# Reordering the head of a two-layer hybrid trunk on one Trainium2 core

## The chip, the core and the metric

The kernel runs on one core of one Trainium2 chip. Its engines run side by side and wait for each other by semaphores: TensorE (PE in the profile; its weight loads are PEld), VectorE (DVE), ScalarE (ACT), GpSimd (POOL) and SyncE (SP), which here issues nearly all DMA loads. The metric is the device time of one execution in microseconds. Lower is better.

## The reference, cut to what matters

The reference is a trunk of two layers on 256 tokens of 1024 channels, all in float32. A vector `c` gives six modulation vectors for each layer; a layer is a token mixer and a convolutional FFN, each on a modulated, normalised input.

```python
for l in range(2):
    mod = c @ mod_w[l] + mod_b[l]            # 6 vectors of 1024
    sh1, sc1, g1, sh2, sc2, g2 = split(mod, 6)
    h = rmsnorm(x, norm1_g[l]) * (1 + sc1) + sh1
    x = x + g1 * mixer(h, positions, ...)    # proj = h @ w_in; rotary embedding; two attentions; gates
    h = rmsnorm(x, norm2_g[l]) * (1 + sc2) + sh2
    x = x + g2 * conv_ffn(h, ...)
return rmsnorm(x, final_g)
```

Only the start of the first layer matters here: the first modulation columns (shift and scale, 128 channels at a time), the sum of squares over the channels of `x`, the modulated input `h`, and its product with the first part of `w_in`. The rotary embedding needs tables of sines and cosines of the positions, and the attentions need masks; both are first used much later, near 50 us.

## The kernel before, in words

Channels lie on the 128 partitions, so `x` is a tile of 8 blocks of 128 channels by 256 tokens. Every float32 product is made of three matmuls at a reduced float format: a high and a low part of each operand, high times high, high times low, low times high (`mm3`). So each weight block that is loaded (`raw`) is split: ScalarE makes the high part (`whi`, an `Identity` activation with rounding, `split_hi`), VectorE the low part (`wlo`, a subtraction, `split`). Likewise the input: `ht` (VectorE) is `x` times gain times the row factor, `hh` (ScalarE) its high part with the shift added, `hl` (VectorE) its low part.

The work is a list of steps (`add(...)`, executed by `run_steps`), each with the weight tiles that it consumes. All weights go through SyncE's queue, in the order of use, into rings of tiles. A load into a tile that was in use waits on that queue until the tile is free. `pin("V", "A", "PE")` keeps the instructions of VectorE, ScalarE and TensorE in the order of the program from there on; without it a scheduler may move them.

The head (the part of the run that the change touches) does this:

- five loads on SyncE: positions, frequencies, a part of the small vectors `vc`, and `x` in two halves; then the weight stream;
- constants by memset and iota; `begin` squares `x` on ScalarE, half by half, and adds the squares on VectorE; `tables` makes the rotary angles with some twenty-five steps of 16 elements on VectorE and two sines on ScalarE; `masks` makes the masks;
- `go0`: modulation column 0. `mod_mm(k, half, raw)` multiplies one half of its rows (eight matmul records on the TensorE timeline), and copies the result out to `mods` after the second half. The sums of the squares over channels are matmuls with a column of ones (`sum_rows`: two matmuls, four records). `rstd` makes the row factor on VectorE and GpSimd (a power). `mod_fin` transposes the column, spreads the row factor over partitions (`rstd_rows`), reduces the column (`modr`), adds the bias (`mod`), makes the gain, and then `ht`, `hh`, `hl` of that block of channels;
- `go(k)`, for k = 0 to 7: the rows of weight block k. Its matmuls come in two halves of tokens (`rows_block` with js = (0,) and (1,): three pairs each, high-high, low-high, and last high-low, which needs `wlo`), then twelve for the other heads (`rows`). Between them stand `mod_fin(k + 1)`, which makes the next block of `h`, the splitting of the next weights, and at the end `mod_both(k + 2)`, a later modulation column.

`go(0)` makes modulation column 1 ahead of its first half:

```python
if k == 0:
    mod_both(1, *mc[:2])
    mc = mc[2:]
...
state["split_hi"](2)
rows_block(S["idx"], k, w, 0, ..., (0,))
mod_fin(k + 1)
rows_block(S["idx"], k, w, 0, ..., (1,))
rows(k, w, 1)
state["split"](2)
if mc:
    mod_both(k + 2, *mc)
```

Of the kernel before, what the change touches and what calls it, by code (L numbers as in the profile page):

```python
# [16 lines left out]
P = 128  # L17
# [10 lines left out]
# buffers: of raw weights, of split weights (pairs), of small work tiles; tiles lent to early loads  # L28
# [4 lines left out]
# how many weight tiles are split ahead of a step  # L33
# [5 lines left out]
# modulation vectors: those summed on the vector engine, those spread over the mixer, over the FFN  # L39
# [4 lines left out]
# parts of a vector that fill the gaps around the norms, and the places of their loads  # L44
# [3 lines left out]
# engines that keep the order of the program between the layers  # L48
# [21 lines left out]
def hybrid_trunk(ctx: ExitStack, tc: tile.TileContext, xT, vec, fbias, pos, invf,  # L70
# [8 lines left out]
    class Engine:  # L79
        """an engine whose instructions stay in the order of the program while pinned"""  # L80
# [42 lines left out]
    # ------------------------------------------------- the stream of weights  # L123
    # steps run in order; the tiles they name are loaded, and split, ahead of them
# [10 lines left out]
    def run_steps():  # L135
        """chunks (source, columns, kind): "w" and "m" pass through the ring "raw", "s" through
        the tiles FIRST and "g", four at a time, through the tile of the gates, both from the
        epoch on that the fourth entry names, and not before the other chunks that stand less than
        the fifth entry behind it"""
# [95 lines left out]
    # ---------------------------------------------------------------- inputs  # L235
# [3 lines left out]
    nc.sync.dma_start(posi, pos)  # L239
    ivf = const.tile([P, 8], F32, name="ivf")  # L240
    nc.sync.dma_start(ivf, invf)
    nc.sync.dma_start(vc[:, :V_L + V_CW], vec[:, :V_L + V_CW])
# [4 lines left out]
    # ------------------------------------------------------------- constants  # L247
# [3 lines left out]
    V.tensor_scalar(ident, jp, 0.0, None, op0=OP.is_equal)  # L251
    tri = const.tile([P, 3 * P], F32, name="tri")
    V.memset(tri[:, 0:P], 0.0)
    V.memset(tri[:, 2 * P:], 1.0)
    causal = const.tile([P, T], F32, name="causal")
    V.memset(causal[:, 0:P], 0.0)
    chunked = const.tile([P, T], F32, name="chunked")
    V.memset(chunked, 0.0)
    V.memset(chunked[0:64, P + 64:], NEG)
# [12 lines left out]
    V.tensor_copy(cpad[:, :, 0], vc[:, V_C:V_C + KT])  # L272
# [4 lines left out]
    V.memset(LF, 0.0)  # L277
    cum = const.tile([P, T], F32R, name="cum")
    V.memset(f(cum), 0.0)
# [19 lines left out]
    def tables():  # L299
        """rotary tables, cos | cos and -sin | sin, one row per token"""  # L300
# [16 lines left out]
        for c in (PI_1, PI_2, PI_3):  # L317
            for n in (nh, nt):
                V.scalar_tensor_tensor(ang, n, -c, ang, op0=OP.mult, op1=OP.add)
        PI = TWO_PI / 2  # L320
# [5 lines left out]
        A.activation(ss[:, :, 8:16], ang, AF.Sin)  # L326
        V.scalar_tensor_tensor(nt, ang, -1.0, ang, op0=OP.mult, op1=OP.min)
        V.tensor_scalar(nt, nt, PI / 2, None, op0=OP.add)
        A.activation(cc[:, :, 0:8], nt, AF.Sin)
# [5 lines left out]
    # ------------------------------------------------------------ modulation  # L335
# [8 lines left out]
    def mod_vector(l, v, kind=(("m",),), vector=False):  # L344
        """one of the six vectors, eight row blocks: summed over the blocks in PSUM, or on the vector
        engine with the last sum over rows in PSUM; a column tile for each 256 columns"""
# [42 lines left out]
    # ---------------------------------------------------------- normalisation  # L389
# [59 lines left out]
    def h_stream(l, rb, shift, hh, hl):  # L449
        """the blocks one after the other, the high part of each ahead of the low part of the one before"""  # L450
        t = h_high(l, 0, rb, shift, hh)
        for k in range(KT):
            n = h_high(l, k + 1, rb, shift, hh) if k + 1 < KT else None
            h_low(l, k, t, shift, hh, hl)
            t = n
            yield
# [7 lines left out]
    def rows_block(tiles, k, w, base, split, hh, hl, js=(0, 1), low_last=False):  # L464
        """one 128-row block of a token-major projection"""
# [770 lines left out]
```

## Time and profile before

| what | us |
|---|---|
| median of 3 runs | 819.35 |
| lowest and highest run | 817.91, 819.90 |
| span of the profiled execution (first to last instruction) | 817.1 |
| TensorE busy in it | 795.0 |
| VectorE, ScalarE, GpSimd busy in it | 643.1, 498.7, 8.9 |

The profiled execution is known by its span alone: no time of its own beyond that is listed. The lowest run is 0.8 us above that span, the median 2.25. Times in the rows are microseconds from the start of the span. A row of the timeline has the start, the duration, the engine, the line of the code (a helper, for nearly all), the operation, the tile that it writes and those that it reads, their shape, and how many instructions were merged into it; in brackets stands how long the engine was idle before and what released it.

### The profile page before, as it was taken

The page shows a single profiled execution, that of the slowest core. Times are in us where ns is not written, and L with a number is a line of the kernel's source. Part 1 is how long each engine was busy: PE and PEld are TensorE (multiplying, and loading weights), DVE is VectorE, ACT ScalarE, POOL GpSimd, SP SyncE. Part 2 cuts the span into 40 slices and gives each one's busy share as a digit, 9 for nine tenths or more (in the row PEclk, how much of TensorE's full clock was granted, in tenths as well). Part 3 has the DMA queues.
Part 4 walks back from the last instruction along what each step waited for, and adds up shares of the span by engine and source line. Part 5 has one row for each costly group of instructions (what it writes and reads, how often), then busy time and mean ns, then how long its engine had stood idle before and what let it go on. Part 6 is the DMA issues. An engine that isn't in the chain of part 4 may idle for free.

```text
span 817.1 us, 16972 instructions
## 1 busy us (share of the span) xinstructions
PE 795.0 (97%) x6644; PEld 758.1 (93%) x6644; DVE 643.1 (79%) x1338; ACT 498.7 (61%) x905; POOL 8.9 (1%) x19
## 2 busy tenths in 40 slices
PE   4999999999999999999999999999999999999997
PEld 2899988989899999999989999999998999999996
DVE  6689998879689998898666799766876877676763
ACT  4476567645476665667654666766555765666664
POOL 2000000000000000000000000000000000000000
PEclk9999999999999999999999999999999999999998
DMA  8955867867969899997525456433693665566611
GB/s 325 409 152 175 282 209 234 261 230 264 413 248 322 314 319 333 322 331 248 168 71 151 140 189 209 128 125 108 196 373 100 210 190 191 185 183 183 193 38 52
DMA packets 51776, 179.24 MB, mean 219 GB/s; under 512 B 6256, under 2 KB 6384, under 8 KB 51696
## 3 DMA queue, kind: packets, MB, share of 16 engines
q1 hardware_dynamic: 51696, 178.15, 64.7%
q8 instruction: 52, 0.85, 0.4%
q14 instruction: 28, 0.23, 0.1%
HBM read 177.08 MB, written 1.05 MB: 218 GB/s over the span
## 4 chain that ended last, share of the span: by engine, by line
PE 51%; issue 24%; DVE 2%; DMA 1%; POOL 0%; ACT 0%; POOLq 0%; DVEq 0%; ACTq 0%
PE psA L89 30%; PE psB L89 19%; PE psM L89 2%; PE psC L89 1%; DVE y L89 1%; DVE wlo L89 1%; DMA raw<-wout 1%; DVE raw L89 0%; POOL rstd L417 0%; ACT whi L89 0%; DVE hl L89 0%; DVE kzl L89 0%; DVE yout L89 0%; POOLq L1231 0%; DVE ql L89 0%
## 5 line engine op out<-in xcount | busy, mean ns | idle before, releaser
L89 DVE TENSOR_TENSOR wlo<-raw,whi 128x1024 fp32r<-128x1024 f32 (+3 forms) x252 | 293.4, 1168 | 79.9 <-ACT whi L89 78.4
L89 ACT ACTIVATE whi<-raw 128x1024 fp32r<-128x1024 f32 (+3 forms) x252 | 254.4, 1014 | 157.4 <-PE psB L89 58.2
L89 PE MATMUL psB<-hh,whi 128*128 128x256 f32 x768 | 215.7, 282 | 0.0
L89 PE MATMUL psB<-hl,whi 128*128 128x256 f32 x768 | 215.4, 281 | 0.0
L89 PE MATMUL psB<-hh,wlo 128*128 128x256 f32 x768 | 215.1, 280 | 0.0
L89 PEld LDWEIGHTS psB<-hh,whi 128*128 128x128 f32 x768 | 144.1, 188 | 2.5 <-issue 1.6
L89 PEld LDWEIGHTS psB<-hl,whi 128*128 128x128 f32 x768 | 144.5, 188 | 0.8 <-DVE hl L89 0.8
L89 PEld LDWEIGHTS psB<-hh,wlo 128*128 128x128 f32 x768 | 144.8, 189 | 0.0
L89 PE MATMUL psA<-hh,whi 128*128 128x256 f32 x448 | 127.7, 286 | 0.0
L89 PE MATMUL psA<-hl,whi 128*128 128x256 f32 x448 | 125.8, 281 | 0.2 <-DVE hl L89 0.2
L89 PE MATMUL psA<-hh,wlo 128*128 128x256 f32 x448 | 125.4, 280 | 0.0
L89 PE MATMUL psA<-gh,wlo 128*128 128x256 f32 x352 | 99.2, 282 | 0.0
L89 PE MATMUL psA<-gh,whi 128*128 128x256 f32 x352 | 99.2, 282 | 0.0
L89 PE MATMUL psA<-gl,whi 128*128 128x256 f32 x352 | 98.9, 281 | 0.0
L89 PEld LDWEIGHTS psA<-hh,whi 128*128 128x128 f32 x448 | 84.1, 188 | 1.9 <-issue 1.7
L89 PEld LDWEIGHTS psA<-hl,whi 128*128 128x128 f32 x448 | 84.3, 188 | 1.1 <-issue 0.4
L89 PEld LDWEIGHTS psA<-hh,wlo 128*128 128x128 f32 x448 | 84.3, 188 | 0.0
L89 DVE SCALAR_TENSOR_TENSOR y<-us,vc,y 128x255 f32<-128x255 f32 (+1 forms) x176 | 76.3, 481 | 5.1 <-ACT y L89 4.8
L89 PEld LDWEIGHTS psA<-gh,whi 128*128 128x128 f32 x352 | 66.4, 189 | 0.4 <-issue 0.4
L89 PEld LDWEIGHTS psA<-gl,whi 128*128 128x128 f32 x352 | 66.2, 188 | 0.1
L89 PEld LDWEIGHTS psA<-gh,wlo 128*128 128x128 f32 x352 | 66.3, 188 | 0.0
L89 ACT ACTIVATE y<-us,vc 128x256 f32<-128x256 f32 x88 | 48.5, 595 | 1.3
(204 smaller groups left out, 1213.5 us busy)
## 6 DMA issues: line engine op xcount, KB each, us to landing
raw<-wup SPq DMA_DIRECT2D x88, 512.0 KB, 4.5
raw<-wmod SPq DMA_DIRECT2D x76, 512.0 KB, 5.4
raw<-wdn SPq DMA_DIRECT2D x44, 512.0 KB, 4.4
raw<-wgate SPq DMA_DIRECT2D x32, 512.0 KB, 4.4
rawg<-wmod SPq DMA_DIRECT2D x20, 512.0 KB, 8.6
raw<-wrow SPq DMA_DIRECT2D x16, 548.0 KB, 5.2
raw<-wbr SPq DMA_DIRECT2D x16, 512.0 KB, 4.0
raw<-wout SPq DMA_DIRECT2D x16, 512.0 KB, 3.6
```

Of the source, the lines that this page charges most:

```text
L89: r = fn(*a, **kw)
```

## The change

The head is put in another order; nothing else in the program is touched. Comments were taken out as well. What it does:

- positions, frequencies and small vectors are loaded from ScalarE's queue, not SyncE's;
- seven memsets (parts of `tri`, `causal`, `chunked`, all of `LF` and `cum`) go from VectorE to GpSimd;
- `tables` is cut into `angles`, `clamp` and the rest. `angles` and the identity stand at the start of `begin`, the copy of `c` into `cpad` behind them, `clamp` between the two halves of the squares. VectorE is pinned in `begin`. The sines with what follows them (`tables`) stand behind `go(2)`, `masks` behind `go(1)`;
- the squares are added on VectorE only in pairs; TensorE sums the four remaining tiles (four `sum_rows`, not one), after both halves of modulation column 0, not between them;
- in `go(0)` the second modulation column (`mod_both(1)`) stands behind the first half of the rows, `mod_fin(1)` behind the second half, and the high part of weight block 1 (`split_hi(2)`) behind `mod_fin(1)`.

```diff
     posi = const.tile([P, 2], I32, name="posi")
-    nc.sync.dma_start(posi, pos)
+    nc.scalar.dma_start(posi, pos)
     ivf = const.tile([P, 8], F32, name="ivf")
-    nc.sync.dma_start(ivf, invf)
-    nc.sync.dma_start(vc[:, :V_L + V_CW], vec[:, :V_L + V_CW])
+    nc.scalar.dma_start(ivf, invf)
+    nc.scalar.dma_start(vc[:, :V_L + V_CW], vec[:, :V_L + V_CW])
...
-    V.tensor_scalar(ident, jp, 0.0, None, op0=OP.is_equal)
     tri = const.tile([P, 3 * P], F32, name="tri")
-    V.memset(tri[:, 0:P], 0.0)
-    V.memset(tri[:, 2 * P:], 1.0)
+    G.memset(tri[:, 0:P], 0.0)
+    G.memset(tri[:, 2 * P:], 1.0)
     causal = const.tile([P, T], F32, name="causal")
-    V.memset(causal[:, 0:P], 0.0)
+    G.memset(causal[:, 0:P], 0.0)
     chunked = const.tile([P, T], F32, name="chunked")
-    V.memset(chunked, 0.0)
-    V.memset(chunked[0:64, P + 64:], NEG)
+    G.memset(chunked, 0.0)
+    G.memset(chunked[0:64, P + 64:], NEG)
...
-    V.tensor_copy(cpad[:, :, 0], vc[:, V_C:V_C + KT])
...
-    V.memset(LF, 0.0)
+    G.memset(LF, 0.0)
     cum = const.tile([P, T], F32R, name="cum")
-    V.memset(f(cum), 0.0)
+    G.memset(f(cum), 0.0)
...
-    def tables():
+    TB = {}
+
+    def angles():
+
         posf = const.tile([P, 2], F32, name="posf")
         V.tensor_copy(posf, posi)
         ang = const.tile([P, 2, 8], F32, name="ang")
...
+        TB["t"] = ang, nt
+
+    def clamp():
+        ang, nt = TB["t"]
         PI = TWO_PI / 2
         V.tensor_scalar(nt, ang, PI, -TWO_PI, op0=OP.is_gt, op1=OP.mult)
...
-        A.activation(ss[:, :, 8:16], ang, AF.Sin)
         V.scalar_tensor_tensor(nt, ang, -1.0, ang, op0=OP.mult, op1=OP.min)
         V.tensor_scalar(nt, nt, PI / 2, None, op0=OP.add)
+
+    def tables():
+
+        ang, nt = TB["t"]
+        A.activation(ss[:, :, 8:16], ang, AF.Sin)
         A.activation(cc[:, :, 0:8], nt, AF.Sin)
         V.tensor_copy(cc[:, :, 8:16], cc[:, :, 0:8])
         V.tensor_scalar(ss[:, :, 0:8], ss[:, :, 8:16], -1.0, None, op0=OP.mult)
...
+    def squares(i):
+        sq = ACC["q"]
+        A.activation(sq[:, i], x[:, 4 * i:4 * i + 4, :], AF.Square)
+
+    def pairs_of_squares(i):
+        sq = ACC["q"]
+        V.tensor_add(sq[:, i, 0:2], sq[:, i, 0:2], sq[:, i, 2:4])
+
     def begin():
-        sq = work.tile([P, 2, 4, T], F32, name="sq0", tag="hl")
-        ACC["s"] = []
+
+        pin("V")
+        ACC["q"] = work.tile([P, 2, 4, T], F32, name="sq0", tag="hl")
+        V.tensor_scalar(ident, jp, 0.0, None, op0=OP.is_equal)
+        angles()
+        V.tensor_copy(cpad[:, :, 0], vc[:, V_C:V_C + KT])
         for i in range(2):
-            A.activation(sq[:, i], x[:, 4 * i:4 * i + 4, :], AF.Square)
-            V.tensor_add(sq[:, i, 0:2], sq[:, i, 0:2], sq[:, i, 2:4])
-            a = work.tile([P, T], F32, name="sqh", tag="t1", bufs=4)
-            V.tensor_add(a, sq[:, i, 0], sq[:, i, 1])
-            ACC["s"].append(a)
-        a, b = ACC["s"]
-        V.tensor_add(a, a, b)
+            squares(i)
+            pairs_of_squares(i)
+            if i == 0:
+                clamp()
...
     add(begin, ahead=0)
-    add(tables, ahead=0)
-    add(masks, ahead=0)
     HH = {}
...
                 mod_mm(0, 0, a)
                 sp = bank("C")
-                sum_rows(sp, ACC["s"][0], True, True)
                 mod_mm(0, 1, b)
+                for i in range(4):
+                    sum_rows(sp, ACC["q"][:, i // 2, i % 2], i == 0, i == 3)
                 r = rstd(sp)
                 state["split_hi"](1)
                 mod_fin(0, r)
...
                 hh, hl = HH["h"]
-                if k == 0:
-                    mod_both(1, *mc[:2])
-                    mc = mc[2:]
                 if k + 1 == KT:
...
-                state["split_hi"](2)
+                if k > 0:
+                    state["split_hi"](2)
                 rows_block(S["idx"], k, w, 0, ((0, 320), (320, 584)), hh, hl, (0,))
-                mod_fin(k + 1)
-                rows_block(S["idx"], k, w, 0, ((0, 320), (320, 584)), hh, hl, (1,))
+                if k == 0:
+                    mod_both(1, *mc[:2])
+                    mc = mc[2:]
+                    rows_block(S["idx"], k, w, 0, ((0, 320), (320, 584)), hh, hl, (1,))
+                    mod_fin(k + 1)
+                    state["split_hi"](2)
+                else:
+                    mod_fin(k + 1)
+                    rows_block(S["idx"], k, w, 0, ((0, 320), (320, 584)), hh, hl, (1,))
                 rows(k, w, 1)
                 state["split"](2)
...
+                if k == 1:
+                    add(masks, ahead=0)
+                if k == 2:
+                    add(tables, ahead=0)
             add(rest)
```

## Rows read from the trace of the kernel before

**Rows 1.** The page's busy time (us, share of the span) and instructions by engine.

```profile
...
PE 795.0 (97%) x6644; PEld 758.1 (93%) x6644; DVE 643.1 (79%) x1338; ACT 498.7 (61%) x905; POOL 8.9 (1%) x19
...
```
**Rows 2.** TensorE's waits: tile, what released it, total us, times, longest.

```profile
...
PE psM L89 <- DMA raw<-wmod: 9.4, 1, 9.4
PE psA L89 <- DVE lg L89: 2.7, 4, 1.1
...
```
**Rows 3.** Timeline of SyncE's queue, 0 to 60 us.

```profile
...
0.74 0.39 SPq L239 DMA_DIRECT2D posi<-pos  x1
...
2.12 0.91 SPq L244 DMA_DIRECT2D x<-xT  x2
...
```
**Rows 4.** DMA issues at 3.6 and at 17.1 us: KB, us to landing.

```profile
...
raw<-wmod SPq DMA_DIRECT2D x1, 512.0 KB, 7.0
...
raw<-wmod SPq DMA_DIRECT2D x1, 512.0 KB, 11.2
```
**Rows 5.** Timeline of TensorE, 9 to 24 us.

```profile
...
9.38 1.08 PE L89 MATMUL psM<-raw,cpad 128*32 128x256 f32 x8 [9.38 <-DMA raw<-wmod]
...
11.83 1.01 PE L89 MATMUL psC<-ones,sqh 128*128 128x1 f32 x4 [1.37 <-DVE sqh L89]
...
12.77 1.08 PE L89 MATMUL psM<-raw,cpad 128*32 128x256 f32 x8
...
14.83 1.06 PE L89 MATMUL psC<-ident,rstd 128*128 128x128 f32 x4
...
15.82 1.94 PE L89 MATMUL psM<-raw,cpad 128*32 128x256 f32 x16
...
18.73 0.54 PE L89 MATMUL psA<-wlo,hh 128*128 128x320 f32 x2
...
19.24 0.52 PE L89 MATMUL psA<-whi,hh 128*128 128x320 f32 x2
...
20.14 0.28 PE L89 MATMUL psB<-hh,whi 128*128 128x256 f32 x1
...
21.66 1.07 PE L89 MATMUL psM<-rawg,cpad 128*32 128x256 f32 x16
...
23.30 0.43 PE L89 MATMUL psA<-wlo,hh 128*128 128x320 f32 x2
...
```
**Rows 6.** Timeline of VectorE, GpSimd and ScalarE, 2 to 23 us.

```profile
...
2.53 0.50 DVE L89 CAST posf<-posi 128x2 f32<-128x2 int32 x1
...
4.43 0.55 POOL L297 MEMSET kzl<- 128x512 f32 x1
...
13.13 0.69 POOL L417 TENSOR_TENSOR rstd<-var,mhalf 128x2 f32<-128x2 f32 x1 [8.14 <-DVE var L89]
...
15.93 0.48 DVE L89 SCALAR_TENSOR_TENSOR ht<-x,gain,psC 128x256 f32<-128x256 f32 x1 [0.30 <-PE psC L89]
...
17.38 1.29 DVE L89 TENSOR_TENSOR wlo<-raw,whi 128x1096 fp32r<-128x1096 f32 x1
...
18.37 1.12 ACT L89 ACTIVATE whi<-raw 128x1096 fp32r<-128x1096 f32 x1 [0.18 <-DMA raw<-wrow]
...
19.52 0.17 DVE L89 TENSOR_REDUCE modr<-psM 128x2 f32<-128x8 f32 x1 [0.85 <-PE psM L89]
...
20.64 0.51 ACT L89 ACTIVATE hh<-ht,mod 128x256 fp32r<-128x256 f32 x1 [1.15 <-DVE ht L89]
...
21.58 1.29 DVE L89 TENSOR_TENSOR wlo<-raw,whi 128x1096 fp32r<-128x1096 f32 x1
...
```
**Rows 7.** Timeline of ScalarE and VectorE around the tables, before and in block 4.

```profile
...
9.08 1.28 ACT L89 ACT_TABLE_LOAD   x1
...
10.73 0.17 DVE L89 COPY cc<-cc 128x16 f32<-128x16 f32 x1 [0.27 <-ACT cc L89]
...
31.73 0.37 ACT L89 COPY mods<-psM 128x256 f32<-128x256 f32 x1 [1.68 <-PE psM L89]
...
32.87 0.17 DVE L89 TENSOR_REDUCE modr<-psM 128x2 f32<-128x8 f32 x1 [1.09 <-PE psM L89]
...
```
## The prediction

> **What bounds the kernel now.** I read the page first: TensorE is busy 795.0 of 817.1 us [rows 1]. Then the waits of TensorE over the whole run: 9.4 us of its idle time lies ahead of its first matmul, and the largest wait anywhere behind the head adds up to 2.7 us, in four pieces [rows 2]. So from about 18 us on the kernel is one long stream of matmuls, and whatever delays or advances its start goes through to the end nearly whole. The change touches only the first 36 us; the question is how much earlier or later this stream reaches, say, the second weight block.
>
> Third I read the timeline of the head. SyncE issues three small loads from 0.74 us and the first half of x at 2.12 [rows 3]. The first modulation column starts at 9.38, as its load lands [rows 5]. The sums of squares start at 11.83, behind a VectorE sum [rows 5]. From there a chain runs through GpSimd's power (13.13 to 13.82), the row broadcast of rstd on TensorE (14.83 to 15.89), the first `ht` at 15.93, `hh`, `hl`, and at last the low part of weight block 0 (`wlo`, 17.38 to 18.67) [rows 5, 6]. The low-part matmuls of block 0 ("low pair" from here) start at 18.73 [rows 5]; the low pair of block 1 follows at 23.30, 4.57 later. These two are my milestones. [...]
>
> **The change part by part.**
>
> *Small loads on ScalarE's queue.* SyncE's first issue is then x, at 0.74 instead of 2.12: 1.38 us earlier [rows 3], and the weight stream behind it moves with it. The first column's halves land at about 7.9 (9.38, less 0.1 and 1.38 [rows 5]) and 9.15 (issued about 3.54, landing 7.0 later [rows 4], less 1.38). On ScalarE the triggers stand ahead of squares that wait for x anyway, so they are free; if the first table load (1.28, as the later one [rows 7]) came ahead of them, `cpad` would come later and cost up to 0.4.
>
> *Memsets to GpSimd.* They free VectorE before 2.5 us, where it then waits for `pos`: worth nothing. A cost is possible: the two-element cast at 2.53 took 0.50, while GpSimd's memsets ran (to 4.98), against 0.17 for a two-element reduction later [rows 6]. The seven memsets that move add some 1.3 us (0.55 for 512 columns), to 6.3. `cpad` now stands behind the sixteen steps of `angles`: from 2.53 at 0.5 a step to 6.3 and at 0.2 after that, it is ready near 8.2. Its load lands at 7.9, but the second half's only at 9.15, so these 0.3 are covered; without that cover they would cost 0.3. [...]
>
> *Squares summed by TensorE.* Removed: three 256-column VectorE adds. Added: three more row sums, twelve more matmul records. Four took 1.01 at half clock including the last one's drain [rows 5], so about 0.22 each (an estimate). They stand behind both halves of the column: 9.15 + 0.1 + 0.9 gives 10.15; sixteen records take 3.5, the drain 0.15: 13.8. VectorE's last pair sum has `clamp`'s seven small steps ahead of it, but x lands 1.38 earlier, and three adds fewer follow than in the chain that ended at 11.8 before; TensorE needs it only at 11.9, behind the first eight records. So the row sums end 0.96 later than the 12.84 of before, although everything ahead of them is earlier. Then 0.98 to the end of the power, and the rstd broadcast with its first weight load, 1.3: `ht` at 16.1 instead of 15.93. What is saved: the second half of the column and its evacuation no longer follow the sums, which gives back the rest. First term: **+0.2 us**. Bounds: +0.6 with the late `cpad`; -2.2 if TensorE were at full clock there (sums 1.75, broadcast 0.65 shorter).
>
> *Second modulation column inside block 1.* (In the code this is step `go(0)`.) Before, its sixteen matmuls ran from 15.82 to 17.7, exactly while `ht`, `hh`, `hl` and `wlo` of block 0 were made: they cost nothing. `wlo` still stands behind `hl` on VectorE, so the low pair of block 0 waits for it as before; the column now comes after it, and nothing hides it. Count from the low pair L: pair and two transposes 0.51 (18.73 to 19.24), column 1.00 (21.66 to 22.66), second half of the rows 0.90 (19.24 to 20.14), and 0.28 to the reduction `modr` (19.24 to 19.52): L + 2.69 [rows 5, 6]. From `modr` to the end of `hh` 1.63 (19.52 to 21.15). Now the moved `split_hi(2)`: the high part of weight block 1 stood ahead of `hh` on ScalarE (18.37, ended 19.49) and now stands behind it: 1.05 more. Only then can VectorE make `wlo` of block 1: 1.29, with 0.1 of hand-overs. The low pair of block 1 comes at L + 6.75, against L + 4.57. Second term: **+2.2 us**, of which 1.0 is the column without cover and 1.2 the late high part (TensorE alone would be there at L + 5.6). Behind TensorE's wait stands the whole stream. Lower bound 1.0, if TensorE is so slow there that the split hides.
>
> *Loads behind that column.* A later column reuses its tiles, so its load waits on SyncE until about 20, and the later rows' loads behind it. Loads of that stretch land 11.2 after their issue [rows 4], so the queue has work throughout: nothing; without that backlog, one wait of about 1.3.
>
> *Masks and tables later.* The masks are six VectorE steps, about 1.15, in a gap of 1.1 that VectorE has in each block: nothing, within `wlo`'s margin. The tables go behind `go(2)`: ScalarE's table load and two sines start after `mods` (31.73 + 0.3 = 32.0), and VectorE's copy of `cc`, which waits for them, keeps `modr` behind it, although its matmuls are done at 32.8. In the old place the copy came 1.65 after the load began (9.08 to 10.73) and the next step could begin 0.2 later; so `modr` moves from 32.87 [rows 7] to 33.85, 0.98 later, and with it `hh` and `wlo` of block 4. `wlo` had a margin: in block 1 it ended at 22.87, its pair began at 23.30, with 0.1 for the hand-over [rows 5, 6]. Third term: 0.98 - 0.33, **+0.65 us**; bounds 0 and 1. In the old place the tables cost nothing, since ScalarE was idle. The row has 1.28 for the load, and only 0.37 from its end (10.36) to the copy, with both sines between. [...]
>
> *Clock.* TensorE had been busy almost without pause from 14.83 to its rise near 18 us. Now it waits about 1 us before `hh` and 0.7 for `wlo` in that stretch. If it rises later, the column (1.94 instead of 1.07) and half the rows run slow: 0 to 1.7. Fourth term: **+0.6**, a third of the upper end.
>
> Sum: 0.2 + 2.2 + 0.65 + 0.6 = **+3.6 us**. The profiled execution has a span of 817.1, so 820.7; the median of the runs is 2.25 above that span, so 822.95.
>
> **The rivals.** [...]
> *Slower still: the clock rises late.* Column and rows of block 0 all at half rate, the fourth term at its upper end: 0.2 + 2.2 + 0.65 + 1.7 = +4.75 (824.1). For it: the two new waits of TensorE before `hh` and `wlo`. Against it: the stretch from 15 us on is still more than half busy.
> *The lead comes through.* If the high part of weight 1 and the sums are hidden after all, what is left is the 1.38 of the loads: 817.95. For it: the first matmul did wait for its load. Against it: the orders on ScalarE and VectorE are pinned.
> *The change does not reach the end,* because a later wait absorbs it: 819.35. Against it: waits behind the head are few [rows 2].
>
> **How the numbers follow.** Forecast 0.50, late clock 0.15, early clock 0.17, lead 0.10, absorbed 0.08. A measurement of this kernel can tell 0.3%, 2.46 us, from no change. The forecast's own range is 1.9 to 4.6 us, nine tenths of it beyond 2.46: slower 0.45 + 0.15 = 0.60. Same: 0.05 + 0.17 + 0.08 and half of the lead, 0.35. Faster 0.05. The range from 817.9 (the lead) to 824.8 (late clock and late `cpad`) leaves out less than 2 in 10.
>
> **What would show it.** Right: the first square starts 1.4 us earlier; row sums of sixteen records end near 13.8; `ht` at 16.1; low pairs at 18.9 and near 25.6 or later; `whi` of block 1 behind its `hh`; a table load near 34 with a TensorE wait for `wlo` behind it. Wrong: sums at 0.11 each, `ht` before 15, or low pairs less than 5.6 apart.

## The result, and the profile after

The change made the kernel slower: median 826.77 us (6 runs, 825.83 to 827.97) against 818.63 for the kernel before (6 runs, 817.04 to 819.90), ratio 1.0095 [1.0080, 1.0109]. The profiled execution took 825.84 with a span of 824.1, 7.0 more than the span before. Forecast was +3.6; the range ended at 824.8.

The page first: TensorE's busy time has grown by 4.3 against [rows 1], with twelve records more.

```profile
span 824.1 us, 16994 instructions
...
PE 799.3 (97%) x6656; PEld 762.4 (93%) x6656; DVE 641.1 (78%) x1328; ACT 499.6 (61%) x905; POOL 10.1 (1%) x26
```

The row sums alone account for 2.6 of it (3.57 here against 1.01 before). The other 1.7 must be matmuls that were there before and last longer. The timeline of TensorE shows which. The rows answer to [rows 5].

```profile
10.04 1.94 PE L89 MATMUL psM<-raw,cpad 128*32 128x256 f32 x16 [10.04 <-DVE cpad L89]
11.90 3.57 PE L89 MATMUL psC<-ones,sq 128*128 128x1 f32 x16
15.34 0.67 PE L89 MATMUL psM<-ident,mods 128*128 128x128 f32 x2
16.52 1.22 PE L89 MATMUL psC<-ident,rstd 128*128 128x128 f32 x4 [0.51 <-POOL rstd L425]
18.85 0.85 PE L89 MATMUL psA<-whi,hh 128*128 128x320 f32 x2 [1.11 <-ACT hh L89]
...
20.58 0.86 PE L89 MATMUL psA<-wlo,hh 128*128 128x320 f32 x2 [0.35 <-DVE wlo L89]
21.36 1.94 PE L89 MATMUL psM<-raw,cpad 128*32 128x256 f32 x16
23.23 0.85 PE L89 MATMUL psA<-whi,hh 128*128 128x320 f32 x2
...
24.85 0.63 PE L89 MATMUL psM<-ident,mods 128*128 128x128 f32 x2
...
26.35 0.41 PE L89 MATMUL psB<-hh,wlo 128*128 128x256 f32 x1
26.56 0.38 PE L89 MATMUL psB<-hh,whi 128*128 128x256 f32 x1
26.77 0.29 PE L89 MATMUL psB<-hl,whi 128*128 128x256 f32 x1
...
29.53 0.54 PE L89 MATMUL psA<-wlo,hh 128*128 128x320 f32 x2 [0.26 <-DVE wlo L89]
```

Three readings. The first matmul no longer waits for its weights but for `cpad`, at 10.04, 0.66 later than before. The low pair of block 0 comes at 20.58 (+1.85), that of block 1 at 29.53: 8.95 apart, not 4.57. And the same 256-column matmul takes 0.41 at 26.35 and 0.29 at 26.77: there TensorE goes from a lower rate to a higher one, against about 18.5 before (the low pair at 18.73 already took 0.54, here 0.86 at 20.58). "Half rate" and "full rate" below are levels of such durations: sixteen modulation matmuls take 1.94 at 21.36 and 1.07 at 27.46, as they do at 15.82 and 21.66 before. The prediction calls the lower level half clock. The granted clock doesn't show it: it is 1.00 in both kernels from 0 to 28 us. It does show a fall between the layers of the kernel before, to 0.51 from 421.1 to 424.6 us, and sixteen matmuls of the same shape take 1.91 there (at 421.09). That a clock makes the level of the head as well is an inference from these like durations; the durations are what tells the level. What TensorE did before the rise: it stood still for 1.11 us before `hh` and 0.35 before `wlo`, then worked without a pause from 20.58 to 26.77.

VectorE, ScalarE and GpSimd, from their timelines, answering to [rows 6]:

```profile
5.08 1.17 DVE L89 CAST posf<-posi 128x2 f32<-128x2 int32 x1 [3.50 <-DMA posi<-pos]
6.73 0.36 DVE L89 TENSOR_SCALAR ang<-ivf,posf 128x8 f32<-128x8 f32 x2 [0.47 <-DMA ivf<-invf]
...
9.82 0.17 DVE L89 COPY cpad<-vc 128x8 f32<-128x8 f32 x1
...
17.77 0.48 DVE L89 SCALAR_TENSOR_TENSOR ht<-x,gain,psC 128x256 f32<-128x256 f32 x1 [1.17 <-PE psC L89]
...
25.52 0.17 DVE L89 TENSOR_REDUCE modr<-psM 128x2 f32<-128x8 f32 x1 [5.00 <-PE psM L89]
...
26.63 0.51 ACT L89 ACTIVATE hh<-ht,mod 128x256 fp32r<-128x256 f32 x1 [2.89 <-DVE ht L89]
27.04 1.10 ACT L89 ACTIVATE whi<-raw 128x1096 fp32r<-128x1096 f32 x1
...
28.18 1.30 DVE L89 TENSOR_TENSOR wlo<-raw,whi 128x1096 fp32r<-128x1096 f32 x1 [0.52 <-ACT whi L89]
```

VectorE stood idle 3.50 us for the positions. The view of DMA issues from 0 to 4 us says why (engine and queue, count, KB, median us from issue to landing):

```profile
raw<-wmod SPq DMA_DIRECT2D x2, 512.0 KB, 7.1
...
vc<-vec ACTq DMA_DIRECT2D x1, 40.0 KB, 6.9
posi<-pos ACTq DMA_DIRECT2D x1, 1.0 KB, 4.3
ivf<-invf ACTq DMA_DIRECT2D x1, 4.0 KB, 5.5
```

On SyncE's queue, ahead of `x`, the same three took 2.3, 1.8 and 1.6, by the same view of the kernel before:

```profile
vc<-vec SPq DMA_DIRECT2D x1, 40.0 KB, 2.3
posi<-pos SPq DMA_DIRECT2D x1, 1.0 KB, 1.8
ivf<-invf SPq DMA_DIRECT2D x1, 4.0 KB, 1.6
```

Beside the two megabytes of `x` and weights that SyncE now issues at once they take 4.3 to 6.9, although they have a queue to themselves. The windows show how busy the core's DMA engines were meanwhile: a mean share of 0.89 to 1.06 in each us from 2 to 9 here, against 0.05 and 0.29 in those from 1 to 2 and 2 to 3 before, while the positions were loaded.

The lead of SyncE's queue reached the weights only in part: the first of them lands 6.7 after its issue at 1.65, at about 8.3, against 9.24 before (3.07 + 6.2). That is 0.9, not 1.38. `x` itself came earlier by more: the first square starts at 4.90, against 6.75 before. Nothing could use it, since the pair sums on VectorE stand behind the late `angles`.

Last, the tables, answering to [rows 7]: the timelines of ScalarE, VectorE and TensorE.

```profile
38.48 1.28 ACT L89 ACT_TABLE_LOAD   x1
...
40.12 0.18 DVE L89 COPY cc<-cc 128x16 f32<-128x16 f32 x1 [1.99 <-ACT cc L89]
...
43.68 0.54 PE L89 MATMUL psA<-wlo,hh 128*128 128x320 f32 x2 [0.54 <-DVE wlo L89]
```

| low pair of block | 0 | 1 | 2 | 3 | 4 | 7 |
|---|---|---|---|---|---|---|
| before | 18.73 | 23.30 | 27.75 | 32.18 | 36.63 | 49.63 |
| after | 20.58 | 29.53 | 34.09 | 38.54 | 43.68 | 56.80 |
| difference | +1.85 | +6.23 | +6.34 | +6.36 | +7.05 | +7.17 |

Nearly all of the loss is made in three places: the head +1.85, block 0 to block 1 +4.38, the tables +0.69. It then goes through to the end: 7.0 in the span. The medians lie 8.1 apart; by the ratio's interval that is 6.5 to 8.9, and 7.0 lies in it. Part of the gap between the two numbers is chance: the profiled execution of the kernel before has a stretch at a granted clock of 0.51 near 421 us that this one lacks. Matmul for matmul (the start of the same matmul in the two traces, counted from the end of the run) the distance is 7.2 ahead of that stretch and 6.6 behind it.

### The profile page after: what moved, and what is told of

It reads as the page before. It is cut to its first block, busy times and chain, and to the rows that moved or that the text cites. A ratio compares the mean times of both kernels' runs of the same rounds, so it can differ in the third digit from the quotient of the medians.

```text
span 824.1 us, 16994 instructions
## 1 busy us (share of the span) xinstructions
PE 799.3 (97%) x6656; PEld 762.4 (93%) x6656; DVE 641.1 (78%) x1328; ACT 499.6 (61%) x905; POOL 10.1 (1%) x26
## 4 chain that ended last, share of the span: by engine, by line
PE 51%; issue 24%; DVE 2%; DMA 1%; POOL 0%; ACT 0%; POOLq 0%; DVEq 0%; ACTq 0%
PE psA L89 29%; PE psB L89 19%; PE psM L89 2%; PE psC L89 1%; DVE y L89 1%; DVE wlo L89 1%; DMA raw<-wout 1%; DVE raw L89 0%; POOL rstd L425 0%; ACT whi L89 0%; DVE hl L89 0%; DVE kzl L89 0%; DVE yout L89 0%; POOLq L1256 0%; DVE ql L89 0%
```

## The experiments

The theory at this point: in the head, the late small loads and with them a late `cpad` cancel the lead; between blocks 0 and 1, half rate adds to the reordering. The rivals: row sums on TensorE alone make the head's loss; the reordering alone makes the 4.38. "Before" and "after" below name the two kernels with the edit shown. Each ratio is to the kernel before, timed on the same chip.

### The head

**Small loads back on SyncE, in the kernel after.**

```diff
-    nc.scalar.dma_start(posi, pos)
+    nc.sync.dma_start(posi, pos)
...
```


> The changed kernel with positions, frequencies and small vectors back on SyncE's queue, ahead of x. Theory of the late small loads: on ScalarE's queue they share the DMA engines with x and land at 5.1, 6.6 and 8.5 us; back on SyncE they land near 2.5, 2.8 and 3.9 again, cpad stands ready near 8 and no longer gates the first column, which then waits for its own load (near 9.3, later again by 1.4). Sums start near 11.5 instead of 11.9, and the time falls by about 0.4 us from 826.8: the lead and the late small loads nearly cancel. Rival (the lead is worth its 1.4 us and the loss lies elsewhere): the time rises by about 1.4.

Measured: 1.0072 [1.0044, 1.0101]; low pair of block 0 at 20.30, 0.28 better than after. The positions land early again, and are of no use. Timeline of VectorE, and under it the last of GpSimd's memsets:

```profile
2.52 3.76 DVE L89 CAST posf<-posi 128x2 f32<-128x2 int32 x1 [0.93 <-DMA posi<-pos]
...
9.40 0.17 DVE L89 COPY cpad<-vc 128x8 f32<-128x8 f32 x1
...
5.73 0.52 POOL L295 MEMSET kzl<- 128x512 f32 x1
```

A cast of two elements takes 3.76 us: it ends with GpSimd's last memset. In the kernel before the same cast fell among eight such memsets too and took 0.50 [rows 6]. So the late loads are not the whole cause: beside the row of memsets on GpSimd, now fifteen long, the cast takes 3.76, and beside eight of them alone 0.57 (next run). By what the one engine holds up the other, and why the cast got in between the memsets in the kernel before and not here, the runs don't show; here and in the kernel after VectorE had been idle just ahead of it. In the kernel after this costs nothing by itself: the cast ends at 6.25, and the frequencies, which the next step needs, land at 6.6.

**The same with the memsets back on VectorE**, so that GpSimd has only its eight.

```diff
-    G.memset(chunked, 0.0)
+    V.memset(chunked, 0.0)
...
```


> The changed kernel with the three small loads back on SyncE and the seven memsets back on VectorE. Theory (VectorE's first cast is blocked as long as GpSimd's memsets run without a gap, 3.76 us with the moved memsets): the cast takes about 0.5 us, as before, cpad is ready by 7.8 instead of 9.4 and the first column starts at 9.35 with its load. Rival (the memsets that clear the keys block it, not the moved ones): the cast still takes over 2 us.

Measured (one run): 823.93, span 822.2; low pair of block 0 at 20.48.

```profile
2.61 0.57 DVE L89 CAST posf<-posi 128x2 f32<-128x2 int32 x1
...
7.25 0.17 DVE L89 COPY cpad<-vc 128x8 f32<-128x8 f32 x1
```

The cast is short again and `cpad` is ready at 7.25, 2.6 earlier than after. But with the small loads first, the column's weights land late, the row sums start at 11.81, and the head has gained 0.1. The long cast is real, and not what sets the end: either the weights or `cpad` is late, and one of them is enough.

**Small loads on ScalarE's queue, in the kernel before.** The edit is the first one's inverse.

> The kernel before with only the three small loads moved to ScalarE's queue. Theory of the late small loads: they land near 5.1, 6.6 and 8.5, x lands 1.4 to 1.8 earlier; the first column starts near 8.7 with cpad, but VectorE's table steps start 2.5 us later and push the square sums, so the block 0 low pair comes within 0.7 us of its 18.7, later or earlier. Rival (the lead of the loads comes through): low pair of block 0 at 17.4 and the time 1.4 us less than before.

Measured: 1.0031 [1.0016, 1.0047]; low pair of block 0 at 20.93 (+2.20), the next at 25.48, 4.55 on. The first column begins at 8.46, 0.92 earlier, and the row sums at 14.03, 2.20 later, since VectorE's steps for the tables, now late, stand among its sums of squares. A miss: within 0.7 was expected. This one edit, which the prediction had as a gain, costs 2.2 in the kernel before.

**Squares summed by TensorE, in the kernel before.**

```diff
-        a, b = ACC["s"]
-        V.tensor_add(a, a, b)
...
+                for i in range(4):
+                    sum_rows(sp, ACC["q"][:, i // 2, i % 2], i == 0, i == 3)
```


> The kernel before with only the sums changed: VectorE adds in pairs, TensorE sums four tiles behind both halves of column 0. Theory (sixteen records at 0.22 us cost more than the three adds that they replace): sums start near 11.4, as both halves have landed by 10.5, and end near 15.0, ht comes near 17.2 instead of 15.9, time 0.8 to 1.4 us over before. Rival (the adds saved pay for it): ht at 15.9 or earlier, time the same or less.

Measured: 1.0018 [1.0000, 1.0036]; low pair of block 0 at 20.29 (+1.56). Timeline of TensorE:

```profile
11.53 3.57 PE L89 MATMUL psC<-ones,sq 128*128 128x1 f32 x16
```

Sixteen records in 3.57, as worked out (3.5). So the prediction's price of the sums was right, and its +0.2 stood on a lead of 1.38 that did not come through: 0.2 + 1.38 is 1.58, against 1.56 here without any lead.

### From block 0 to block 1

**The new order of `go(0)` alone, in the kernel before.** The edit is the part of the diff that changes `go(0)`.

> The kernel before with only the new order in go(0). Theory (order): the low pair of block 0 stays at 18.7, that of block 1 comes 6.75 later if the clock rises near 18 us, up to 9 later if it rises late; time 2.2 to 4.4 us over before. Rival (the loss needs the late head of the change): under 1 us over before.

Measured: 1.0050 [1.0031, 1.0069]; low pairs at 18.73 and 27.69, 8.96 apart as in the kernel after (8.95). This part alone is enough for the 4.38. Timeline of TensorE:

```profile
18.73 0.85 PE L89 MATMUL psA<-wlo,hh 128*128 128x320 f32 x2 [0.36 <-DVE wlo L89]
19.52 1.94 PE L89 MATMUL psM<-raw,cpad 128*32 128x256 f32 x16
```

The low pair at the same 18.73 now runs at 0.85 instead of 0.54: it is still at half rate. In the kernel before, the column filled the time in which `ht`, `hh` and `wlo` are made, and TensorE came out of it at full rate (the next low pair, at 19.87, took 0.43; here, at 22.52, 0.69).

**The old order of `go(0)`, in the kernel after.** The inverse.

> The changed kernel with the old order in go(0): second column ahead of the rows, high part of weight 1 ahead of hh. Theory (order of go(0) costs the distance of the low pairs, 8.95 against 4.57 us): the distance is 4.6 to 5.2 and the time 3.7 to 4.4 us less than the 826.8 of the change. Rival (the late clock makes the loss by itself): the clock still rises near 26 us, the distance stays over 7 and the time falls by 2 at most.

Measured: 1.0047 [1.0031, 1.0063]; low pairs at 20.86 and 26.29, 5.43 apart: 3.5 of the 4.38 come back, with a first pair still at 0.77 for two. That is a little less than expected (4.6 to 5.2 apart). The head stays late.

**The column moved, the high part left in its old place, in the kernel before.**

```diff
-                    mod_fin(k + 1)
-                    state["split_hi"](2)
+                    state["split_hi"](2)
+                    mod_fin(k + 1)
```


> The kernel before with the second column moved behind the first half of the rows and mod_fin(1) behind the second, as in the change, but with the high part of weight 1 still ahead of hh. Theory (at half clock TensorE hides the late high part, so that it costs 0.4 us, and the column and the clock cost the rest): distance of the low pairs 8.4 to 8.6. Rival (my prediction's split, 1.0 for the column and 1.2 for the late high part): distance near 7.8.

Measured: 1.0039 [1.0024, 1.0053]; low pairs at 18.49 and 26.16, 7.67 apart, 1.29 less than with both moved (8.96). That is near the 1.2 that the prediction gave for the late high part (the rival here), but it doesn't isolate it: the rate rose earlier than with both moved, as the last pair of the second half tells (0.43 for two at 22.07 here, 0.69 at 22.52 there), although TensorE's work up to there is the same. So the rise also differs from one execution to the next.

**Five throw-away matmuls in the pause behind the row factor's broadcast**, with the new order of `go(0)`, in the kernel before.

```diff
                     S["rb"] = rstd_rows(r=rs)
+                    idle_mm(S["fox"][1][:, 1, :], 5)
```


> The kernel before with the new order in go(0), and five extra matmuls on a constant tile, whose result is thrown away, in TensorE's pause between the rstd broadcast and the first rows. Theory (the pause that the moved column leaves delays the clock's rise, and the late clock is half of the loss): with the pause filled the clock rises by 20.6 us, and the low pairs of blocks 0 and 1 lie 6.8 to 7.8 us apart, not 8.96; time 1 to 2 us below the unfilled one (823.9). Rival (the moved column alone, whatever the clock): distance within 0.4 of 8.96.

Measured: 1.0026 [1.0010, 1.0042]; low pairs 8.37 apart. Inconclusive: the low pair of block 0 and the column still ran at half rate (0.86, 1.94), the rate rose only behind them (the second half's last pair took 0.43, not 0.69), and 0.59 of the distance came back, between the theory and its rival. One filled pause did not bring the early rise back.

**Throw-away matmuls from the start, in the kernel before**: 40 from 1.19 us on, on constants, and 8 and 3 behind the halves of the first column.

```diff
+        idle_mm(wb[:, :T], 40)
```


> The kernel before with throw-away matmuls on a constant tile: forty from the start, eight behind the first half of column 0, three behind the second. Theory (the head of the kernel before runs at half clock, and TensorE's own steps in it cost twice): the clock rises before 9 us and stays, the four records of the row sums take 0.5 instead of 1.01 and the rstd broadcast 0.6 instead of 1.06, ht comes near 14.6 instead of 15.93, the block 0 low pair near 17.4, and the time falls by 1.0 to 1.6 us. Rival (the chain is bound by VectorE and the loads): low pair within 0.4 of 18.73, time the same.

Measured: 0.9995 [0.9977, 1.0013]. The head itself does gain: full rate by the first column (eight records in 0.64, not 1.08), row sums 0.60 instead of 1.01, low pair of block 0 at 17.31 (-1.42), of block 1 at 21.85 (-1.45). Block 2 then waits for its load, and its low pair comes at 26.71, 1.04 earlier than before. No gain is left in the time. Matmul for matmul, this run is still 1.0 ahead of the kernel before at 100 us, and 0.8 behind it from 200 us on. The largest step lies at 103.5 us, in the attention. ScalarE and TensorE there, first in the kernel before, then in this one:

```profile
97.79 1.06 ACT L89 ACTIVATE whi<-raw 128x1024 fp32r<-128x1024 f32 x1 [1.48 <-DMA raw<-wqkf]
...
103.52 0.38 PE L89 MATMUL psC<-ident,X 128*128 128x128 f32 x2
```
```profile
98.58 1.06 ACT L89 ACTIVATE whi<-raw 128x1024 fp32r<-128x1024 f32 x1 [3.31 <-DMA raw<-wqkf]
...
103.67 0.44 PE L89 MATMUL psC<-ident,X 128*128 128x128 f32 x2 [1.03 <-DVE X L89]
```

A block of weights comes 0.8 later than before, though it was issued 1.0 earlier (6.7 from issue to landing, 4.9 before). VectorE's `wlo` and `X` stand behind it, TensorE waits 1.03 for `X`, and the lead is gone. A second loss stands in the windows (us, busy time and count of PE, PEld, DVE, ACT, POOL, granted clock, DMA share, GB/s). The first line is the kernel before, the second this one:

```profile
416.00:430.00 14.00, 13.76 (x128) 10.04 (x127) 9.25 (x17) 8.41 (x13) 1.75 (x1) 0.88 0.29 84
```
```profile
416.00:430.00 14.00, 13.78 (x118) 9.69 (x118) 8.76 (x16) 8.56 (x14) 1.75 (x1) 0.76 0.21 60
```

Between the layers the granted clock falls, to 0.51 from 421.1 to 424.6 us in the kernel before. The shares lost, 0.12 and 0.24 of 14 us, come to about 3.4 us in the profiled execution before and 6.7 in this one (an estimate, with a level of one half for both); the kernel after has 1.00 there. By the same count the longer fall costs this run 1.6 more than the kernel before. Whether it comes and how long it is differs between the profiled executions.

**The same warm start with the new order of `go(0)`** and nine more matmuls in the pause.

> The same throw-away matmuls, nine more behind the rstd broadcast, and the new order in go(0). Theory (my sum for go(0) was right for full clock, and the clock made up the rest of the 8.95 us): the low pairs of blocks 0 and 1 lie 6.5 to 6.9 apart; time 2 us over the run with the throw-away matmuls and the old order. Rival (the loss has another cause than the clock): distance over 8.

Measured: 1.0014 [0.9994, 1.0034]. Timeline of TensorE:

```profile
17.55 0.54 PE L89 MATMUL psA<-wlo,hh 128*128 128x320 f32 x2 [0.68 <-DVE wlo L89]
18.02 1.07 PE L89 MATMUL psM<-raw,cpad 128*32 128x256 f32 x16
...
24.35 0.54 PE L89 MATMUL psA<-wlo,hh 128*128 128x320 f32 x2 [0.53 <-DVE wlo L89]
```

At full rate the two low pairs lie 6.80 apart; the prediction's sum, made of durations at full rate, was 6.75. This settles the split: of the 4.38, 2.2 are the order itself (6.80 - 4.57; the old order at full rate, in the run above, has 4.54) and 2.15 the half rate (8.95 - 6.80).

### The tables

**Tables and masks back behind `begin`, in the kernel after.**

```diff
     add(begin, ahead=0)
+    add(tables, ahead=0)
+    add(masks, ahead=0)
```


> The changed kernel with the tables and masks back behind begin. Theory (the sines behind go(2) make modr of block 4 wait): the low pairs of blocks 3 and 4 lie 4.45 apart instead of 5.14, and nothing is lost in the head, since the last square sums are no later. Rival: the distance stays 5.1, or the head loses more than 0.7.

Measured (one run): 823.89, span 822.1, 2.0 below after's. The low pairs of blocks 3 and 4 lie 4.44 apart (38.25, 42.69) and not 5.14, with no TensorE wait between 30 and 45 us; the head lost 0.1 (low pair of block 0 at 20.69). The third term is confirmed at 0.7. Of the rest of the 2.0, 0.4 is a block 1 that follows block 0 at 8.56 and not 8.95, and 0.9 comes between 60 and 200 us; from one run neither can be put down to the tables.

### Can the lead be had at all?

**A leaner head, on the kernel before**: `x` first on SyncE, with `vc` between its halves; positions and frequencies on ScalarE's queue; masks and angles in VectorE's gaps between the first blocks, sines behind the last `hh`; weight block 0 split early.

> A version drawn from the findings, built on the kernel before: x's first half leads SyncE's queue, small vectors behind it, second half; positions and frequencies on ScalarE's queue, as nothing early needs them now; masks, the angle steps (five at a time) and the table copies in VectorE's gaps behind go(0) to go(6), the sines behind the last hh; sums, order of go(0) and memsets as before; the split of weight 0 ahead of the second half of column 0. Theory (with the small loads of no consequence the lead is worth what it promises): row sums start near 10.6 instead of 11.83, ht near 14.7, the block 0 low pair near 17.5; time 1.0 to 1.4 us less than before. Rival (the lead is lost on the way): low pair at 18.5 or later, time the same.

Measured: 1.0005 [0.9987, 1.0024]; low pairs at 17.84 (-0.89) and 22.83 (-0.47). The second half of `x` landed where it had before, three small loads having come in beside it, and block 1 waited for its weights. A miss.

**`lean2`: both halves of `x` ahead of `vc`, no early split.**

```diff
-    nc.sync.dma_start(vc[:, :V_L + V_CW], vec[:, :V_L + V_CW])
     for i in range(2):
         nc.sync.dma_start(x[:, 4 * i:4 * i + 4, :], xT[:, 4 * i:4 * i + 4, :])
+    nc.sync.dma_start(vc[:, :V_L + V_CW], vec[:, :V_L + V_CW])
...
+                if k == 6:
+                    sines()
```


> The kernel before with only the lead that the change aimed at: on SyncE the two halves of x, then vc, then the weights; the two small loads of the tables leave ScalarE's queue inside block 0, behind the second half's copy of block 1; masks, angles and sines stand in VectorE's and ScalarE's pauses between the first blocks; the order inside block 0 and the squares stay as before. If late small loads, the longer row sums and the pauses in block 0 are all that stood between the change and its lead: ht near 13 us (before 15.93), the low pairs of blocks 0 and 1 near 16 and 20.2 (before 18.73 and 23.30), and a time 2.5 to 3 us below before, ratio 0.9965. If the lead is taken by the other loads again, or by the weight rows of block 1, or by the clock's half level that lasts longer when work starts earlier: low pair of block 1 at 22 or later and a time within 0.5 us of before.

Measured: 1.0004 [0.9990, 1.0017]. One thing was not as announced: the two small loads left ScalarE's queue at 0.73 after all. The head does what was hoped, low pairs at 16.52 and 21.10 (-2.21, -2.20), and still at -2.16 in block 7 (47.47). But the time is the same. The timeline of ScalarE at the end of the stage shows the first part of the way down:

```profile
45.70 1.28 ACT L89 ACT_TABLE_LOAD   x1
...
47.22 2.52 ACT L89 ACTIVATE whi<-raw 128x1024 fp32r<-128x1024 f32 x3
```

In the kernel before, these high parts begin at 47.75: with the sines ahead of them the lead is 0.53 there, about 1.2 in the low parts after them, and 1.46 in TensorE's next product, at its first matmul with `wlo` (the kernel before, then `lean2`):

```profile
51.91 0.28 PE L89 MATMUL psA<-hh,wlo 128*128 128x256 f32 x1
```
```profile
50.45 0.28 PE L89 MATMUL psA<-hh,wlo 128*128 128x256 f32 x1
```

Matmul for matmul, 1.3 is left of the lead at 120 us and 0.4 from 200 us on. The rest goes in small waits of TensorE in the attention, the longest 0.7 for VectorE's `hl` near 196 us (0.2 before).

**`lean2_warm`: the same with the throw-away matmuls** (36, 5 and 3).

> The same, with 36 throw-away matmuls on constants from the start of TensorE's work and 5 and 3 more in the two pauses of block 0, so that the clock's record is at full before the first row sums; this work is no part of the reference. If half clock is what is left of the head's cost: the low pairs near 15 and 19.2, the time 3 to 4 us below before, 1 below the kernel without the throw-away matmuls. If the loads of the weight rows bound by then: low pairs less than 0.5 earlier than without them and the same time within 0.4 us.

Measured: 0.9992 [0.9978, 1.0006]; low pairs at 15.33 and 20.50 (-3.40, -2.80), 25.37 in block 2 (-2.38), 47.36 in block 7 (-2.27, against -2.16 without the throw-away matmuls). Timeline of ScalarE, the high part of block 2:

```profile
22.07 1.12 ACT L89 ACTIVATE whi<-raw 128x1096 fp32r<-128x1096 f32 x1 [2.25 <-DMA raw<-wrow]
```

It waits 2.25 us for its weights. From there on the loads have taken the higher rate's gain back: a head that is 3.4 us early runs into the weight stream, and is 2.4 early two blocks later.

**`lean3`: lean2 with the sines one block earlier**, in ScalarE's wait of 1.7 us for the column's sums. The angle steps and the copies of the tables move up one block with them.

```diff
-                if k == 6:
+                if k == 5:
                     sines()
```


> lean2 with the table load and the sines one block earlier on ScalarE, behind the copy of the second half of block 6, where the trace of before shows ScalarE idle 1.7 us for the sums of the next column, instead of in front of the three weight copies at the end of the stage. lean2's lead of 2.2 us at the low pairs fell to 1.2 at the first low part behind those copies. If the sines made that: the lead is still near 2.0 at 57 us, and the time is 0.5 to 1.5 us below lean2 and before; of the rest, loads may take up to 0.9 more, since the weights land only 1.3 us earlier than in before. If the loads behind block 7 took it: the lead is 1.2 there again, and the time as lean2's.

Measured: 817.65 (12 runs) against 819.61 for the kernel before on that chip (17 runs), 0.9978 [0.9961, 0.9994]. It is the only version here whose interval lies below 1. Timelines of ScalarE and, behind the last "...", of TensorE at the end of the stage:

```profile
41.47 1.28 ACT L89 ACT_TABLE_LOAD   x1
...
42.89 0.20 ACT L89 ACTIVATE cc<-nt 128x16 f32<-128x16 f32 x1
43.15 0.37 ACT L89 COPY mods<-psM 128x256 f32<-128x256 f32 x1
...
49.97 0.28 PE L89 MATMUL psA<-hh,wlo 128*128 128x256 f32 x1
```

The table load and the sines fit into the wait, `mods` follows at 43.15 (45.10 before, -1.95), and TensorE's next product comes 1.94 earlier than before, as expected, against 1.46 in `lean2`. The median is 2.0 below before's, more than the 0.5 to 1.5 expected; the span is 814.9, 2.2 below. So the same sines cost `lean2` up to 0.7 of its lead and `lean3` nothing. They are not the whole difference: `lean3`'s lead holds in the attention (2.7 from 200 us on) where `lean2`'s falls to 0.4. Whether that follows from the sines isn't shown, and the two intervals of the ratio overlap by a little.

## Why the prediction was wrong

The sign was right (slower 0.60), the size not: 7.0 in the span against 3.6. Two terms of the sum failed, the first and the fourth. The upper end of the range, 824.8, is also 0.3 more than the two bounds that it names add up to (817.1 + 2.25 + 4.75 + 0.4 = 824.5); the measured median, 826.77, is beyond either.

**First term, +0.2: measured +1.85.** The step that failed is the time of `cpad`, "ready near 8.2", and with it the lead of 1.38. That time counts VectorE's steps "from 2.53", when the positions were at hand in the kernel before, with their load first on SyncE's queue, and "at 0.5 a step" beside GpSimd's memsets. Neither held. The triggers on ScalarE were free, as said (they end at 2.10, and the first square still waited 1.48 for `x`, to 4.90); what was left out is the landing of what they load. The positions landed 4.3 after their issue, not 1.8, the frequencies 5.5, so that VectorE's second step began at 6.73 and `cpad` was ready at 9.82. With the loads first on SyncE again it came at 9.40, since the first cast then took 3.76 beside the memsets; with both undone it came at 7.25. So the sums began at 11.90 and not at 10.15, which is 1.75 late; the term missed 1.65. A smaller part is the weights: the column's second half landed at 9.6, not 9.15, so that with `cpad` in time the sums would have begun near 10.6 (an estimate by the prediction's own sum, 9.6 + 0.1 + 0.9). All later prices held: sums 3.57 (3.5 given), from their end near 15.5 to `ht` at 17.77 2.3, as from 13.8 to 16.1. Summing squares on TensorE costs 1.56 by itself. So of the term's two parts, 1.58 for the sums and a lead of 1.38 to pay for them, the first held and the second did not come through in any run with the order of the change.

On the memsets the prediction saw a cost and put it too low. It took 0.50 for a step of VectorE beside GpSimd's memsets, from the one cast in [rows 6]. In `a_small_sp` the same cast took 3.76 and ended with the last of eight memsets of 0.52 each.

**Fourth term, +0.6 (bounds 0 and 1.7): measured 2.2.** The step that failed is the size: "a third of the upper end", and that end itself. The prediction had the right place, a late rise of the rate behind TensorE's new waits before `hh` and `wlo` (1.11 and 0.35 measured). The low pair with what follows to the column took 0.78 instead of 0.51 (20.58 to 21.36), the column 1.87 instead of 1.00, the second half 1.62 instead of 0.90, and the transposes to `modr` 0.67 instead of 0.28: 0.27 + 0.87 + 0.72 + 0.39 = 2.25. The upper bound had the column and the second half of the rows (1.7) and left out the low pair and the transposes; the rate rose behind all four. The late-clock rival had a chance of 0.15 and still fell short by 0.55. That was no accident of one execution: the new order of `go(0)` gave 8.96, 8.96, 8.71 and 8.56 in four other runs without throw-away matmuls (`b_go0_new`, `a_small_sp`, `a_sp_dve`, `a_tables_old`), so that half rate costs 1.8 to 2.2 beyond the 6.80. That the two waits by themselves hold the rate down is not shown: with the first of them filled, TensorE was still at half rate at 21.54 (0.86 for two).

**Second term, +2.2: right.** 6.80 at full rate against 6.75. The column without cover and the late `whi` are both in the trace (`whi` at 27.04 behind `hh` at 26.63; `wlo` at 28.18, released by `whi`). How the 2.2 divides into 1.0 and 1.2 no run isolates.

**Third term, +0.65: right**, 0.69, by the mechanism given: the copy of `cc` waits for ScalarE, `modr` stands behind it, and the low pair of block 4 waits 0.54 for `wlo`. Masks and SyncE's waits cost nothing, as said: no wait of TensorE stands between the low pairs of blocks 1 and 3.

**Rivals.** The early clock, 0.17 of the chances, did not come: the sixteen row sums took 3.57, 0.22 each. No run has them at full rate; four took 0.60 in `b_warm` and 1.01 before. Nothing absorbed the delay. The lead does exist, as `lean3` shows, but not in this order; and `b_warm`, `lean2` and `lean2_warm` show that a lead can be lost further on.

**Open** stays why the load of `wqkf` took longer in `b_warm`, why `lean3` keeps its lead through the attention and `lean2` does not, and what, beside the two waits or in their place, delays the rise of the rate in the new order.

## What to carry to other kernels

Moving the small loads to another queue freed the issuing engine, not the transfer: `x` was issued 1.38 earlier, and the positions took 4.3 to land, not 1.8. Put a small load ahead of the big ones if something early needs it, and follow its landing, not its issue, to the first instruction that reads it. Work that only fills another engine's pause may be worth more than its own time: with the column in the pause TensorE came out of it at full rate near 18.5 us, without it at some point between 22 and 27. Before moving such work, price everything that would then run at half rate up to the new rise. A table load with its sines, 1.62 in all, cost nothing in ScalarE's wait of 1.7 in `lean3`; in two other places it cost TensorE 0.69 (the kernel after) and up to 0.7 (`lean2`), so give each step a place by the waits of the trace. And a lead in the head is worth only what the later loads and waits leave of it (2.2 in the head of `lean2`, 0.4 from 200 us on): follow it, matmul for matmul, past the stage that was changed.

## What the runs showed of the hardware

- Three loads of 1 to 40 KB on ScalarE's queue landed 4.3 to 6.9 us after their issue beside 512 KB loads on SyncE's; ahead of them on one queue 1.6 to 2.3.
- A cast of two elements on VectorE took 0.50 among GpSimd's memsets in the kernel before (they went from 0.52 to 0.55 each) and 3.76 in `a_small_sp`, where VectorE had been idle for 0.93 ahead of it and it ended with the last of them.
- TensorE rose from half to full rate (1.94 and 1.07 for sixteen modulation matmuls) near 18.5 us where it had been busy almost without pause from 14.35 on, and near 26.7 where pauses of 1.11 and 0.35 lay in the stretch. Where throw-away matmuls ran from 1.19 on, eight modulation matmuls took 0.64 in the first column, at 9.35, against 1.08 before. Row sums that kept TensorE busy for 3.57 us were followed by matmuls at half rate (two transposes in 0.67 at 15.34, against 0.38 at 19.11 before). The granted clock was 1.00 in both kernels from 0 to 28 us.
- A fall of the granted clock between the layers, to 0.51 from 421.1 to 424.6 us in the kernel before, came in some profiled executions and not in others (mean granted clock from 416 to 430 us 0.88, 0.76 or 1.00). The one in the kernel before (about 3.4 us) cost its execution 0.6, the one in `b_warm` (about 6.7 us) 2.2, by the same matmuls ahead of it and behind it in a run without one.
